# First writes to a shared stretch of SBUF placed behind the block products, and a slack test before VectorE leaves an operation to another engine

## The chip, the cores and the metric

One Trainium2 chip; the kernel runs on one of its cores. A core has five engines with a queue of their own each: TensorE (PE in the profile, its weight loads PEld), VectorE (DVE), ScalarE (ACT), GpSimd (POOL) and SyncE (SP), which issues the transfers between DRAM and SBUF here. The metric is the device time of one launch in microseconds (us); lower is better. All times are of this one core.

## The reference

One inference step of a two-layer decoder trunk, for a prompt of 512 tokens and 8 sample sequences of one token each, model width 1024, feed-forward width 4096, float32. Cut to what matters here:

```python
for l in range(DEPTH):                       # 2 layers
    u = x @ w_in[l]                          # 1024 -> 1536 columns
    A = window_attention(q, k, v)            # window 128, 8 query heads, 2 kv heads, width 512
    B = recurrent_branch(xr, gr)             # conv, RG-LRU gates, scan, width 256
    C = pool_branch(zp)                      # trailing means, width 256
    x = layer_norm(ALPHA * x + concat(A, B, C) @ w_out[l], ln1_g[l], ln1_b[l])
    x = layer_norm(ALPHA * x + square(relu(x @ w_ff1[l])) @ w_ff2[l], ln2_g[l], ln2_b[l])
```

The prompt and the sample tokens go through the same weights. The caches, shifted by one position, are outputs too.

## The kernel before, in words

**Data.** Activations lie transposed, channels on the 128 partitions and tokens along the free axis, in two halves of tokens: h=0 with 256 columns and h=1 with 256 prompt columns and the 8 samples (264). Each float32 operand of a matmul is split into a high and a low part of the fast type fp32r (`xh` and `xl`, `hh` and `hl`, two halves of a slot `w`). A product of 128 output channels is then three matmuls for each 128 input channels: high with high, low with high, high with low. Weights come by SP into two raw buffers (`raw_93`, `raw_95`), are rounded to the high part by ScalarE and subtracted by VectorE (`w<-raw,w`), and lie in seven slots `w_84` to `w_90`.

**Stages.** Each layer runs the input projection with attention, recurrence and pooling beside it, then the output projection (`do_out`, 8 chunks of 128 channels for each half), the first norm, then the feed-forward in four quarters, f1 and f2 in turn, and the second norm, whose chunks come out of the last f2. Eight pairs of f1 column blocks in a layer (`PAIRS`) are computed by 2 x 2 block products with seven instead of eight products (`do_pair`): sums of input blocks are made as fp32r and the products are combined afterwards by VectorE (`acc`, `ra`).

**The norm** (class `Norm`) takes the chunks as they come. `acc` adds them up (`acc<-y`, `acc<-acc,y`); the squares are added in two running sums. After the fourth chunk a matmul of `acc` with a matrix of 1/1024 (`x<-acc,onesm`) gives a first mean, which is then subtracted from all chunks; after the eighth a second such matmul gives the rest of the mean and `s<-over_f,onesm` the mean square. Then the chunks are normalised and split into `xh` and `xl` (`split`), or stored (`store`). In the first norm of a layer half h=0 is normalised while PE is at half h=1, and h=1 while PE is already at f1 of h=0.

**The shared stretch.** 8384 columns of SBUF have two names, `over_f` (float32) and `over_r` (fp32r). By its first name it holds, in the regions P, Q1, V, KZ, p4, long, gl0 and gl1, scratch of attention and norms: KZ is the zero-padded key buffer, which `layer_start` clears by two GpSimd MEMSETs of 64x512 at the start of each layer; "long" takes, among others, the bias of the last norm, loaded by SP in `Norm.prepare` (`over_f<-in_ln_b_dram`). By its second name it holds the input sums of the block products, in four parts T1 to T4 which cover all of it: 0 to 2112, 2112 to 4224, 4224 to 6336 and 6336 to 8384.

**Order.** Nothing is issued while the program is written down: class `Plan` records every operation (`add`), finds which earlier operations it depends on from the regions that each reads and writes, and then `order` makes a list schedule: every engine takes, from what is ready on its modelled clock, the operation with the lowest rank (the latest start that keeps the estimated end). `issue` emits them in that order, each engine keeps it as its own queue, and the waits between engines are added when the operations are emitted. As each operation is emitted from `issue`, all of them have line L319. Some operations may run on more than one engine: `either` gives an add VectorE and GpSimd, `copy` gives a ScalarE copy one or both of the others. Who takes such an operation is decided in `pick`, inside `order`: `o.eng` is the engine it was written for, `e` the one that is choosing, `free[...]` when an engine's clock is free, `o.rank + late - start` the slack. MARGIN is 3.0 us and BUSY 0.3 us.

## Time and profile before

| | before |
|---|---|
| median of 3 runs | 1107.15 us (1103.31 to 1110.06) |
| the profiled execution | 1105.39 us, its span 1103.3 us |
| mean granted TensorE clock | 0.995 |
| PE busy | 1075.4 us, 97% of the span |
| DVE busy | 796.4 us, 72% |
| ACT busy | 552.4 us, 50% |
| POOL busy | 209.6 us, 19% |

The span is the time from the first to the last instruction on the core; 2.1 us lie around it. A row of the timeline gives start, duration, engine, line, operation, out<-in, shapes, and in brackets how long the engine was idle ahead of it and who ended that. A row of the waits gives engine and operation, whom it waited for, us in total, times, and the longest.

### The profile page before, as it was taken

Reading aid. Unit: us, or ns where it says so; the run is one execution under the profiler, and the core shown is the slowest. Engines: PE = TensorE matmul, PEld = TensorE weight load, DVE = VectorE, ACT = ScalarE, POOL = GpSimd, SP = SyncE. Lnnn points to the kernel's source line nnn. Section 1 sums busy time; section 2 is a strip of 40 time slices with the busy share of each in tenths; the row PEclk is TensorE's granted clock in tenths of the full one; section 3 lists DMA queues with packets and bytes.
Section 4 is the critical chain, followed back from the end, with each engine's and each line's share of the span. In section 5 each row is a group of like instructions: output and inputs, shape, how many; then the busy total and the mean of one; then the engine's idle time right before and its main releaser. Section 6 shows DMA issues by size and latency. Waiting matters only on the chain.

```text
span 1103.3 us, 21246 instructions
## 1 busy us (share of the span) xinstructions
PE 1075.4 (97%) x8541; PEld 1046.6 (95%) x8541; DVE 796.4 (72%) x1661; ACT 552.4 (50%) x1066; POOL 209.6 (19%) x352
## 2 busy tenths in 40 slices
PE   8999999999999999999999999999999999989997
PEld 7988898999999999999998899999999999989996
DVE  5747769999559548669874596799975774675666
ACT  6658755755124224237476776566532431343343
POOL 4334334210000000022242443223000000002103
PEclk9999999999999999999999999999999999999999
DMA  9330413634313422434534040346242242242431
GB/s 266 98 76 3 114 44 116 192 120 137 111 60 98 132 77 78 124 106 155 172 89 99 1 116 5 115 144 205 77 128 67 75 153 77 78 134 83 148 116 40
DMA packets 120021, 116.58 MB, mean 106 GB/s; under 512 B 4481, under 2 KB 118171, under 8 KB 119875
## 3 DMA queue, kind: packets, MB, share of 16 engines
q1 hardware_dynamic: 119570, 115.16, 34.2%
q8 instruction: 67, 1.10, 0.4%
q14 instruction: 32, 0.25, 0.1%
q0 software_dynamic: 352, 0.06, 0.0%
HBM read 112.72 MB, written 4.84 MB: 107 GB/s over the span
## 4 chain that ended last, share of the span: by engine, by line
PE 80%; DVE 7%; ACT 5%; DMA 4%; issue 2%; SPq 1%; POOL 0%; DVEq 0%; ACTq 0%; POOLq 0%
PE mm L319 62%; PE s L319 9%; PE t L319 7%; PE x L319 2%; DVE y L319 2%; DVE over_f L319 2%; DMA raw<-in_w_ff_dram 2%; ACT L319 1%; DVE w L319 1%; DMA raw<-in_w_out_dram 1%; SPq L319 1%; ACT over_f L319 1%; ACT w L319 1%; DMA over_f<-in_x_sample_dram 1%; DVE ra L319 1%
## 5 line engine op out<-in xcount | busy, mean ns | idle before, releaser
L319 PE MATMUL mm<-hh,w 128*128 128x264 f32 (+1 forms) x2496 | 465.6, 285 | 0.8 <-ACT hh L319 0.8
L319 PE MATMUL mm<-xh,w 128*128 128x264 f32 (+1 forms) x2048 | 403.2, 290 | 1.0 <-ACT xh L319 0.9
L319 PEld LDWEIGHTS mm<-hh,w 128*128 128x128 f32 x2496 | 391.9, 190 | 2.8 <-ACT hh L319 1.4
L319 PE MATMUL mm<-hl,w 128*128 128x264 f32 (+1 forms) x1248 | 354.8, 285 | 0.4 <-DVE hl L319 0.4
L319 PEld LDWEIGHTS mm<-xh,w 128*128 128x128 f32 x2048 | 325.9, 190 | 7.1 <-issue 3.8
L319 ACT CAST w<-raw 128x1024 fp32r<-128x1024 f32 (+1 forms) x202 | 209.1, 1041 | 244.7 <-PE mm L319 204.8
L319 PE MATMUL mm<-xl,w 128*128 128x264 f32 (+1 forms) x1024 | 297.0, 290 | 0.0
L319 DVE TENSOR_TENSOR w<-raw,w 128x1024 fp32r<-128x1024 f32 (+1 forms) x202 | 247.5, 1231 | 56.6 <-ACT w L319 53.7
L319 PEld LDWEIGHTS mm<-hl,w 128*128 128x128 f32 x1248 | 237.2, 190 | 1.2 <-DVE hl L319 0.8
L319 PEld LDWEIGHTS mm<-xl,w 128*128 128x128 f32 x1024 | 194.2, 190 | 3.9 <-issue 3.4
L319 DVE TENSOR_TENSOR y<-y,mm 128x256 f32<-128x256 f32 (+1 forms) x96 | 40.5, 422 | 77.7 <-PE mm L319 77.4
L319 ACT CAST hh<-rb 128x264 fp32r<-128x264 f32 (+1 forms) x128 | 50.9, 410 | 54.6 <-DVE rb L319 54.3
L319 POOL TENSOR_SCALAR w<-four 128x512 fp32r<-128x512 f32 x4 | 2.6, 640 | 376.0 <-DVE four L319 376.0
L319 DVE TENSOR_TENSOR hl<-rb,hh 128x264 fp32r<-128x264 f32 (+1 forms) x128 | 52.4, 424 | 8.6 <-ACT hh L319 8.6
L319 PE MATMUL s<-over_r,w 128*128 128x264 f32 x384 | 53.0, 286 | 5.7 <-DMA over_f<-in_ln_b_dram 4.3
L319 PEld LDWEIGHTS s<-over_r,w 128*128 128x128 f32 x384 | 49.1, 189 | 6.3 <-DMA over_f<-in_ln_b_dram 4.6
L319 PE MATMUL t<-over_r,w 128*128 128x264 f32 (+1 forms) x384 | 51.1, 282 | 0.0
L319 PEld LDWEIGHTS t<-over_r,w 128*128 128x128 f32 x384 | 48.0, 188 | 0.0
L319 ACT CAST w<-four 128x1024 fp32r<-128x1024 f32 (+1 forms) x28 | 24.2, 866 | 41.2 <-PE mm L319 26.3
L319 ACT ACT_TABLE_LOAD x32 | 41.1, 1283 | 3.0 <-DVE nm L319 1.7
L319 ACT ACTIVATE over_f<-y 128x264 f32<-128x264 f32 (+1 forms) x49 | 19.4, 418 | 41.5 <-DVE y L319 30.0
L319 ACT ACTIVATE ra<-mm 128x256 f32<-128x256 f32 (+1 forms) x64 | 24.3, 384 | 29.9 <-PE mm L319 29.7
(288 smaller groups left out, 1346.7 us busy)
## 6 DMA issues: line engine op xcount, KB each, us to landing
raw<-in_w_ff_dram SPq DMA_DIRECT2D x80, 1024.0 KB
raw<-in_w_in_dram SPq DMA_DIRECT2D x7, 1024.0 KB
raw<-in_w_in_dram SPq DMA_DIRECT2D x8, 512.0 KB
raw<-in_w_out_dram SPq DMA_DIRECT2D x8, 512.0 KB
raw<-in_w_out_dram SPq DMA_DIRECT2D x16, 256.0 KB
y<-in_x_prompt_dram SPq DMA_DIRECT2D x4, 256.0 KB
raw<-in_w_in_dram SPq DMA_DIRECT2D x4, 256.0 KB
y<-in_x_prompt_dram SPq DMA_DIRECT2D x2, 512.0 KB
```

The lines of the kernel that those rows point to most:

```text
L319: o.ins = fn(*args, **kw)
```

## The change

Two edits.

The first is in `Plan.add`. An operation that touches the stretch under its second name (`over_r`) is remembered, and every later operation that writes the stretch under its first name gets the remembered one, the last recorded use of `over_r`, as one more dependency in the plan, whether their regions overlap or not.

The second is in `pick`. When an engine looks at an operation written for another engine, it passes over it if that other engine is free within 0.3 us. For VectorE this now holds only if the operation also has more than 3 us of slack; an urgent one it may take.

```diff
         self.alias, self.large = {}, False
+        self.second = {}
...
                 rl.append((r, op))
+            if a.name in self.alias:
+                self.second[nm] = op
+            elif w and nm in self.second:
+                deps.add(self.second[nm])
         deps.discard(op)
...
                         if e == "G":
                             if o.rank + late - start < o.alts[e][1] + MARGIN:
                                 continue
-                        elif max(free[o.eng], est) <= start + BUSY:
+                        elif max(free[o.eng], est) <= start + BUSY and (e != "V" or o.rank + late - start > MARGIN):
                             continue
```

The program has as many PE and SP instructions as before, 20 VectorE instructions more, 19 GpSimd instructions and one ScalarE instruction fewer. Three places show what moved.

PE at the last block product of layer 0, before. `t_123` and `s_144` are PSUM banks, `over_r` the input sums, `w_87` and `w_88` weight slots; in brackets the engine whose signal the instruction waits for:

```order
L319 MATMUL t_123<-over_r,w_87 128x264 x12
L319 MATMUL s_144<-over_r,w_88 128x264 [waits DVE_49]
L319 MATMUL s_144<-over_r,w_88 128x264
L319 MATMUL s_144<-over_r,w_88 128x264 [waits Pool_49]
L319 MATMUL s_144<-over_r,w_88 128x264 x6
L319 MATMUL s_144<-over_r,w_88 128x264 [waits Pool_49]
L319 MATMUL s_144<-over_r,w_88 128x264 x2
```

And in the changed kernel:

```order
L319 MATMUL t_123<-over_r,w_87 128x264 x12
L319 MATMUL s_144<-over_r,w_88 128x264 [waits DVE_49]
L319 MATMUL s_144<-over_r,w_88 128x264 x11
L319 MATMUL mm_130<-xh_113,w_86 128x256
L319 MATMUL mm_130<-xl_115,w_86 128x256
```

The matmuls are the same; the two waits for GpSimd, whose MEMSETs of KZ stood between them, are gone.

PE at the last block product of layer 1, before:

```order
L319 MATMUL t_122<-over_r,w_85 128x256 x12
L319 MATMUL s_144<-over_r,w_90 128x264 [waits Activation_49]
L319 MATMUL s_144<-over_r,w_90 128x264
L319 MATMUL s_144<-over_r,w_90 128x264 [waits DMAHW5_49]
L319 MATMUL s_144<-over_r,w_90 128x264 x9
```

In the changed kernel ten of the twelve stand in one row of eleven without a wait for a transfer. SP at the same place, as a difference:

```order
 L319 DMA raw_95<-in_w_ff_dram 128x8x256
 L319 DMA raw_93<-in_w_ff_dram 128x8x256
+L319 DMA raw_95<-in_w_ff_dram 128x8x256
 L319 DMA over_f<-in_ln_b_dram 128x1024
-L319 DMA raw_95<-in_w_ff_dram 128x8x256
 L319 DMA raw_93<-in_w_ff_dram 128x8x256
 L319 DMA raw_95<-in_w_ff_dram 128x8x256
```

The load of the bias stands one weight load later.

VectorE in the first norm of layer 0, before. `y_0_92` and `xh_113`, `xl_115` are of half h=0, which is being normalised, `y_0_94` and `acc_157` of half h=1, whose chunks are still coming, `pcol_98` holds gains and biases:

```order
L319 TENSOR_TENSOR y_0_92<-y_0_92,over_f 128x256
L319 SCALAR_TENSOR_TENSOR over_f<-y_0_92,pcol_98,over_f 128x256 x2
L319 CAST xh_113<-over_f 128x256
L319 TENSOR_TENSOR w_84<-raw_93,w_84 128x1024
L319 SCALAR_TENSOR_TENSOR xl_115<-over_f,pcol_98,xh_113 128x256
L319 SCALAR_TENSOR_TENSOR over_f<-y_0_92,pcol_98,over_f 128x256 x2
L319 TENSOR_TENSOR w_85<-raw_95,w_85 128x1024
L319 SCALAR_TENSOR_TENSOR xl_115<-over_f,pcol_98,xh_113 128x256
L319 TENSOR_TENSOR w_86<-raw_95,w_86 128x1024
L319 SCALAR_TENSOR_TENSOR over_f<-y_0_92,pcol_98,over_f 128x256
L319 SCALAR_TENSOR_TENSOR xl_115<-over_f,pcol_98,xh_113 128x256
L319 TENSOR_TENSOR acc_157<-acc_157,y_0_94 128x264
```

And in the changed kernel, from the first of two adds to the second:

```order
L319 TENSOR_TENSOR acc_157<-acc_157,y_0_94 128x264
L319 SCALAR_TENSOR_TENSOR over_f<-over_f 128x256
L319 TENSOR_TENSOR y_0_92<-y_0_92,over_f 128x256
L319 SCALAR_TENSOR_TENSOR over_f<-over_f 128x256
L319 TENSOR_TENSOR y_0_92<-y_0_92,over_f 128x256
L319 SCALAR_TENSOR_TENSOR over_f<-over_f 128x256
L319 TENSOR_TENSOR y_0_92<-y_0_92,over_f 128x256
L319 SCALAR_TENSOR_TENSOR over_f<-y_0_92,pcol_98,over_f 128x256
L319 COPY y_0_94<-mm_130 128x264
L319 TENSOR_TENSOR acc_157<-acc_157,y_0_94 128x264
```

The last add ahead of the first mean stood behind three weight splits (`w_84` to `w_86`); now it stands ahead of them, and VectorE makes the copy before it, which ScalarE made.

PE at the same place, as a difference (`x_149` is the bank of the mean, `mm_128` an output chunk):

```order
 L319 MATMUL mm_128<-hh_0_126,w_86 128x264 x2
 L319 MATMUL mm_128<-hl_0_127,w_86 128x264
+L319 MATMUL x_149<-acc_157,onesm_100 128x264
 L319 MATMUL mm_128<-hh_0_126,w_86 128x264 x2
 L319 MATMUL mm_128<-hl_0_127,w_86 128x264
```

The first mean matmul of half h=1 is the 1107th matmul on PE instead of the 1168th, 61 earlier; the second, at the end of the chunks, is the 1212th instead of the 1259th, 47 earlier. Layer 1 has the same moves.

Elsewhere: the four copies of the sample caches to the output (`out_dram<-in_cache_k_dram` and three more) stand one weight load earlier on SP in both layers; in whole, the adds `acc<-acc,y` of 128x264 are 5 on GpSimd and 19 on VectorE, which were 16 and 8.

## The prediction

> **What bounds the kernel now.** I read the page's totals first, then PE's waits, then the timeline at each long wait, and at last busy time and clock by stretch.

> ```profile
> span 1103.3 us, 21246 instructions
> PE 1075.4 (97%) x8541; PEld 1046.6 (95%) x8541; DVE 796.4 (72%) x1661; ACT 552.4 (50%) x1066; POOL 209.6 (19%) x352
> PE 80%; DVE 7%; ACT 5%; DMA 4%; issue 2%; SPq 1%; POOL 0%; DVEq 0%; ACTq 0%; POOLq 0%
> ```

> TensorE (PE) is busy for 1075.4 of 1103.3 us and carries 80% of the chain that ended last. The change takes no matmul away, so it can win only from the 27.9 us in which PE is idle and from stretches in which PE's clock is low. Who ends PE's idle time:

> ```profile
> PE x L319 <- DVE acc L319: 6.4, 5, 1.8
> PE s L319 <- DMA over_f<-in_ln_b_dram: 4.3, 1, 4.3
> PE t L319 <- DMA y<-in_x_prompt_dram: 3.6, 1, 3.6
> PE t L319 <- DVE over_f L319: 1.7, 2, 1.1
> PE s L319 <- POOL over_f L319: 1.3, 2, 0.7
> ```

> The columns are us in total, times, longest. Rows two and five (block products `s<-over_r` that wait for something written to `over_f`) are what the first edit speaks to: 5.6 us. Row one (mean matmuls `x<-acc` that wait for VectorE's sum) is what the second edit can reach. Rows three and four stand at the start and in the sample attention, whose work neither edit shortens.

> **Edit 1, the ordering.** In layer 0's last block product two MEMSETs of KZ come between the matmuls:

> ```profile
> 443.96 0.52 POOL L319 MEMSET over_f<- 64x512 f32 x1 [22.27 <-PE s L319]
> 444.54 1.13 PE L319 MATMUL s<-over_r,w 128*128 128x264 f32 x7 [0.70 <-POOL over_f L319]
> 445.73 0.52 POOL L319 MEMSET over_f<- 64x512 f32 x1 [1.24 <-PE s L319]
> 446.30 0.64 PE L319 MATMUL s<-over_r,w 128*128 128x264 f32 x3 [0.63 <-POOL over_f L319]
> ```

> PE reads, POOL writes, PE reads on: each MEMSET is one wait. In the new order both MEMSETs stand behind the last product, and the matmuls have no wait on POOL. That frees 0.70 + 0.63 = 1.33 us. KZ is wanted only by the next layer's attention, after the f2 pass that begins here, and POOL is idle for 22.27 us ahead of the first, so what they cost there is hidden; without that cover it would be 2 x 0.52 = 1.04 us.

> In layer 1 it is the DMA of the ln2 bias:

> ```profile
> 984.24 0.35 SPq L319 DMA_DIRECT2D over_f<-in_ln_b_dram  x1
> 988.50 1.94 PE L319 MATMUL s<-over_r,w 128*128 128x264 f32 x10 [4.34 <-DMA over_f<-in_ln_b_dram]
> 984.30:988.50 4.20, 0.00 (x0) 0.00 (x0) 1.43 (x4) 1.45 (x2) 0.00 (x0) 1.00 0.69 188
> 989.30:992.70 3.40, 3.40 (x18) 3.40 (x17) 2.22 (x4) 1.05 (x1) 0.00 (x0) 0.50 0.41 143
> 993.00:997.00 4.00, 4.00 (x35) 4.00 (x35) 3.37 (x8) 1.71 (x3) 0.00 (x0) 1.00 0.16 32
> ```

> The last three rows are stretches: length, then busy time of PE, PE's weight loads, DVE, ACT, POOL, then granted clock, DMA share, GB/s. PE does nothing for 4.2 us, and then runs 3.4 us at a granted clock of 0.50: 18 matmuls, where the pitch of the next stretch (4.00/35 = 0.114 us) would give 30. Twelve matmuls are lost, 12 x 0.114 = 1.4 us. If the stall goes, I expect the low clock to go with it: 4.34 + 1.4 = 5.74 us. [...]

> The bias load moves behind one weight load on SP's queue, and waits there for the last block product; no matmul stands behind it. The bias is used when the output is stored, at the end of the f2 pass that begins here, and the one weight load that stood behind it is now issued ahead of it. Cost 0; if SP's next load were held up by it, at most about the 4.2 us that PE now stands still for it.

> Edit 1 together: 1.33 + 5.74 = 7.1 us, the upper end; the lower is the stalls alone, 1.33 + 4.34 = 5.7.

> **Edit 2, the slack rule.** So far VectorE (DVE) passed over another engine's operation whenever that engine was soon free; now it does so only where the operation has over 3 us of slack, and takes urgent ones. In the first norm of each layer VectorE gains 6 instructions and POOL loses 5 (among them three adds to `acc_157`), and the mean matmuls stand 61 and 47 matmuls earlier on PE. Here is what they wait for now:

> ```profile
> 178.50 0.68 PE L319 MATMUL x<-acc,onesm 128*128 128x264 f32 x2 [0.98 <-DVE acc L319]
> 191.31 0.71 PE L319 MATMUL x<-acc,onesm 128*128 128x264 f32 x2 [1.40 <-DVE acc L319]
> 714.20 0.68 PE L319 MATMUL x<-acc,onesm 128*128 128x264 f32 x2 [0.97 <-DVE acc L319]
> 727.35 0.71 PE L319 MATMUL x<-acc,onesm 128*128 128x264 f32 x2 [1.75 <-DVE acc L319]
> 160.00:195.00 35.00, 32.56 (x259) 31.67 (x257) 31.84 (x57) 19.72 (x39) 14.63 (x14) 1.00 0.34 107
> 195.00:255.00 60.00, 59.40 (x496) 58.99 (x494) 58.44 (x116) 38.93 (x79) 9.97 (x9) 1.00 0.50 160
> ```

> The most that can be won is 0.98 + 1.40 + 0.97 + 1.75 = 5.1 us. VectorE is busy 31.84 of 35 us there and 58.44 of the next 60, so it is nearly the bound itself. Does the sum come sooner? It depends on where it stands in VectorE's queue:

> ```profile
> 163.31 0.42 DVE L319 TENSOR_TENSOR over_f<-s,over_f 128x256 f32<-128x256 f32 x1
> 163.64 0.62 DVE L319 TENSOR_TENSOR y<-y,over_f 128x256 f32<-128x256 f32 x1
> 165.97 0.81 POOL L319 TENSOR_TENSOR acc<-acc,y 128x264 f32<-128x264 f32 x1 [1.10 <-DVE y L319]
> 166.08 0.97 DVE L319 TENSOR_TENSOR y<-y,over_f 128x256 f32<-128x256 f32 x1
> 168.57 0.36 ACT L319 COPY y<-mm 128x264 f32<-128x264 f32 x1
> 177.93 0.42 DVE L319 TENSOR_TENSOR acc<-acc,y 128x264 f32<-128x264 f32 x1
> 179.73 1.22 DVE L319 TENSOR_TENSOR w<-raw,w 128x1024 fp32r<-128x1024 f32 x1
> 188.01 0.94 POOL L319 TENSOR_TENSOR acc<-acc,y 128x264 f32<-128x264 f32 x1
> 190.84 0.42 DVE L319 TENSOR_TENSOR acc<-acc,y 128x264 f32<-128x264 f32 x1
> ```

> The fourth chunk of y, the last that the first mean needs, was copied by 168.93 and added only at 177.93: the add stood behind nine us of weight splits and other norm work in VectorE's queue. In the new order the add is the 11th instruction behind the variance step (163.31 now), which has two more ahead of it than now. The pitch is 0.33 us (163.31 to 163.64). So the step starts at 163.31 + 0.66 = 164.0, and with two instructions stretched by 0.97 - 0.42 = 0.55 the add starts at 164.0 + 11 x 0.33 + 1.1 = 168.7 and ends at 169.2. PE came to the mean at 178.50 - 0.98 = 177.52. A matmul takes 60/496 = 0.121 us in the stretch from 195, so 61 fewer in front bring PE there at 177.52 - 7.4 = 170.1: 0.9 us to spare.

> For the second mean PE came at 191.31 - 1.40 = 189.91, and comes 47 x 0.121 = 5.7 sooner, less the 0.98 won: 183.2. The squares and adds now run on POOL until 188.95 and on VectorE until 191.26, among weight splits (w, 1.22 each). In the new order 29 small instructions and one split stand between the first mean's add and the last add of the second: 169.2 + 29 x 0.33 + 1.2 and, as a guess, four stretched by 0.55, gives 182.2: 1.0 us to spare. Layer 1's order is the same.

> What it costs VectorE: an add takes 426 ns on VectorE and 816 on POOL, and operations of one shape are stretched where POOL works beside them:

> ```profile
> L319 POOL TENSOR_TENSOR acc<-acc,y 128x264 f32<-128x264 f32 x16 | 13.1, 816 | 15.9 <-DVE y L319 14.2 <-DVE acc L319 1.7
> L319 DVE TENSOR_TENSOR over_f<-over_f 128x264 f32<-128x264 f32 x15 | 11.9, 794 | 0.0
> L319 DVE TENSOR_TENSOR acc<-acc,y 128x264 f32<-128x264 f32 x8 | 3.4, 426 | 0.3
> ```

> Six more instructions are 6 x 0.33 = 2.0 us; five fewer on POOL give back at most 5 x (794 - 426) = 1.8. VectorE comes out even, within its 3.16 + 1.56 = 4.7 us of idle time in 160 to 255. [...]

> Both margins are about 1 us on chains of a dozen instructions, and one stretched instruction takes 0.55 of it. I take two thirds of 5.1: 3.5 us. The ends: 5.1 gained, or a loss, priced with the rivals.

> The other moves: four copies of the sample caches to the output stand one weight load earlier on SP.

> ```profile
> 228.20 0.63 SPq L319 DMA_DIRECT2D out_dram<-in_state_conv_dram  x1
> 249.47 0.38 SPq L319 DMA_DIRECT2D raw<-in_w_ff_dram  x1
> ```

> No load is issued for 21 us behind them, so the displaced load has room: 0. In layers' ends and attention a handful of casts change engine, each some 0.4 us off PE's path: 0, within 1 us either way.

> **Sum.** 7.1 + 3.5 = 10.6 us. The profiled execution took 1105.39 us (span 1103.3 and 2.1 around it): 1094.8. The median of the three runs is 1107.15, 1.8 higher: 1096.6. I predict 1095.5, between them.

> **Rivals.**
> Only edit 1 pays: the sums come sooner, but PE, which meets them sooner too, waits as long as now. Then 1105.39 - 7.1 = 1098.3, or 1100.1 by the median. For it: VectorE 91 to 97% busy there. Against: the 9 us in which the finished chunk lay unused.

> The other side: PE takes its instructions in order, and the mean matmuls stand 61 and 47 earlier. If VectorE finishes the sums only when it does now, PE waits 7.4 + 5.7 = 13.1 us more per layer: 1105.39 - 7.1 + 26.2 = 1124.5. The gain of edit 1 is used up when the sums come 3.5 us per layer behind PE beyond today's waits; slower by 0.5% (5.5 us) needs 6.3. It would take, say, the six new instructions at 1 us each with none of the idle time usable. For it: instructions near 1 us do occur (0.97 above). Against: the queue position as counted.

> The ordering does nothing, because something else holds the same matmuls (a sum from VectorE, a weight): then only edit 2, 1105.39 - 3.5 = 1101.9. Against: VectorE has gaps and PE waits for nothing else in those rows.

> The clock drops elsewhere. It does now, once, after short gaps:

> ```profile
> 666.49 0.24 PE L319 MATMUL t<-ident,over_f 64*128 64x64 f32 x1 [0.64 <-DVE over_f L319]
> 668.50:671.80 3.30, 3.30 (x15) 3.01 (x14) 1.90 (x5) 0.68 (x2) 1.24 (x3) 0.50 0.00 0
> ```

> [...]

> **How the numbers follow.** Both edits pay, 1091.5 to 1098: 0.58. Only edit 1, 1098 to 1101.5: 0.22. The means give back most or all of it, 1101.5 to 1112: 0.12. Beyond that, slower: 0.04. Ordering without effect: 0.04. Best case 1105.39 - 7.1 - 5.1 - 1.4 = 1091.8, and 1.5 lower for the spread of runs: low 1090.3. High 1102: it takes in edit 1 alone by the median (1100.1) with one clock drop more. A measurement of this kernel can tell about 0.5%, 5.5 us, from no change: faster holds the first two cases but for their edge, 0.78; same 0.17; slower 0.05.

> **What would show it.** In the new profile no wait of `s<-over_r` for POOL or for the bias load; no granted clock of 0.50 behind the last block product of layer 1; `x<-acc` waits down from 6.4 to under 3 us in total; the VectorE adds `acc<-acc,y` 128x264 from 8 to 19 and POOL's from 16 to 5. PE's busy time stays near 1075 less the slow stretch. The prediction is wrong if `x<-acc` waits grow past 6.4, if waits for `hh`, `hl` or `w` appear from 195 on, or if weight loads (`raw`) come late and end PE's idle time.

## The result, and the profile after

The changed kernel took 1097.64 us (median of 7 runs, 1094.60 to 1103.00), the kernel before 1105.24 us in the same comparison (7 runs, 1103.18 to 1111.38): a ratio of 0.9927, 95% interval 0.9902 to 0.9952, so 0.5 to 1.0% faster. Times and ratios in this text leave out two single executions far from all others, 3716.55 us of e9 and 1303.65 us of e10. The profiled execution took 1097.64 us, with a span of 1095.9. In its code the line of every operation is L324, in the kernels of the last experiments L335.

Totals and PE's waits of the changed kernel:

```profile
PE 1073.0 (98%) x8541; PEld 1045.8 (95%) x8541; DVE 796.4 (73%) x1681; ACT 550.3 (50%) x1065; POOL 195.2 (18%) x333
...
PE t L324 <- DMA y<-in_x_prompt_dram: 4.8, 1, 4.8
PE mm L324 <- ACT hh L324: 4.1, 2, 2.5
PE mm L324 <- ACT xh L324: 1.8, 1, 1.8
PE t L324 <- DVE over_f L324: 1.3, 2, 0.7
PE s L324 <- DVE nm L324: 1.2, 1, 1.2
PE mm L324 <- DVE hl L324: 1.1, 3, 0.6
PE x L324 <- ACT rb L324: 1.1, 1, 1.1
```

Both groups of waits that the edits speak to are gone: no `s<-over_r` that waits for POOL or for the bias, no `x<-acc` that waits for VectorE. Of the five such waits of before (6.4 us) four were at the first norms and are gone (5.1); the fifth, in the last norm of the kernel (1.32 us, at 1090.86 in before), is still there with 1.08 us, and now stands under ScalarE (`x<-ACT rb`). At the start of f2 two others have grown: `mm` for `hh` and for `hl`, which were in before:

```profile
PE mm L319 <- ACT hh L319: 0.8, 2, 0.4
PE mm L319 <- DVE hl L319: 0.4, 2, 0.2
```

The two last block products, layer 0 and layer 1, in the timeline:

```profile
445.71 1.49 PE L324 MATMUL s<-over_r,w 128*128 128x264 f32 x11
...
982.37 1.63 PE L324 MATMUL s<-over_r,w 128*128 128x264 f32 x12
983.38 0.37 SPq L324 DMA_DIRECT2D raw<-in_w_ff_dram  x1
984.08 0.35 SPq L324 DMA_DIRECT2D over_f<-in_ln_b_dram  x1
```

The twelve matmuls run through, and the bias is issued behind them. Where the new waits stand, by stretches of 3.41 us (PE, its weight loads, DVE, ACT and POOL busy, clock, DMA share, GB/s):

```profile
737.24:740.65 3.41, 3.33 (x28) 3.09 (x26) 3.41 (x7) 3.41 (x7) 0.00 (x0) 1.00 0.68 228
740.65:744.06 3.41, 0.66 (x3) 0.30 (x2) 2.65 (x6) 2.66 (x6) 1.87 (x1) 1.00 0.52 182
744.06:747.47 3.41, 3.10 (x14) 3.10 (x15) 3.23 (x5) 2.29 (x5) 3.38 (x3) 0.50 0.38 128
```

This is the start of f2 in layer 1: PE is nearly idle for a stretch (0.66 us busy of 3.41), and then has half its clock for another (0.50 from 744.06 to 747.47).

To see where time comes and goes, I compare the start of the n-th matmul in two traces. Each trace has 8541 of them, and outside the places that were reordered the same number is the same work. A stage's entry is what the difference to the trace of before changed by between two such numbers (us, negative is gained). The numbers that bound the stages are 0 to 800 (start), 800 to 1200 (sample attention of layer 0), 1200 to 1460 (means), 1460 to 1800 (start of f2), 3300 to 3600 (last block product), 5000 to 5300, 5300 to 5660 and 5660 to 6000 (the same three of layer 1), 7500 to 7900 (the bias). "All" is for the last matmul; the stretches that have no column make up the rest.

| trace | start | sample 0 | means 0 | f2 0 | MEMSETs | sample 1 | means 1 | f2 1 | bias | all |
|---|---|---|---|---|---|---|---|---|---|---|
| changed kernel | 2.44 | 1.31 | -3.26 | 1.78 | -1.91 | -1.49 | -3.38 | 4.15 | -6.15 | -8.14 |
| e1 edit 1 | 1.30 | -0.27 | -0.19 | -0.01 | -1.91 | -1.57 | -0.50 | -0.04 | -6.15 | -9.32 |
| e2 edit 2 | 0.88 | -0.36 | -3.25 | 3.57 | -0.01 | 3.01 | -3.37 | 1.99 | -0.23 | -0.14 |
| e3 both | 0.15 | -0.43 | -3.25 | 2.89 | -1.91 | -1.65 | -3.37 | 1.82 | -6.15 | -13.33 |
| e4 GpSimd's only | 1.03 | 1.35 | -1.31 | 0.04 | -1.91 | 0.15 | -2.80 | 1.00 | -6.15 | -9.91 |
| e5 bias only | 0.23 | 1.85 | -0.17 | -0.01 | 0.00 | -0.01 | 0.62 | -0.04 | -6.15 | -5.12 |
| e6 MEMSETs only | 0.48 | -0.32 | 0.13 | -0.01 | -1.91 | -1.45 | -0.56 | -0.04 | 0.95 | -2.65 |
| e7 half a bias | 0.27 | 1.39 | -0.26 | -0.03 | 0.00 | -0.19 | -0.62 | -0.02 | 0.41 | 1.55 |
| e8 tail first | -0.09 | -0.09 | -3.30 | 0.13 | -1.91 | -1.47 | -3.40 | 0.04 | -6.15 | -15.54 |
| e9 edit 1, tail | 1.48 | -0.27 | -0.19 | 0.84 | -1.91 | -1.13 | -0.58 | 0.83 | -6.15 | -8.34 |
| e10 as e8 | 0.95 | 0.31 | -3.26 | 0.25 | -1.91 | 3.34 | -3.38 | -0.16 | -6.15 | -8.88 |
| e11 e4 with tail | 0.86 | 4.96 | -1.73 | 0.02 | -1.91 | -1.07 | -2.88 | 1.22 | -6.15 | -8.31 |

Two columns repeat to the hundredth wherever edit 1 is whole, MEMSETs and bias; the means repeat within 0.05 wherever edit 2 is whole. The sample columns do not: they swing from -1.65 to 4.96, and between two traces of one kernel too (-1.47 in e8, 3.34 in e10). That is chiefly the granted clock (in the second sample column three windows at 0.50 in e10, none in e8), at the end of this text. Of the stretches without a column one shows edit 2 as well: between 3600 and 5000, at the start of layer 1, the traces with it gain 0.76 to 1.02 us, those without it are between -0.42 and 0.28.

### The profile page after: what moved, and what is told of

Its sections match the earlier page's. It is cut to its first block, busy times and chain, and to the rows that moved or that the text cites. A ratio compares the mean times of both kernels' runs of the same rounds, so it can differ in the third digit from the quotient of the medians.

```text
span 1095.9 us, 21224 instructions
## 1 busy us (share of the span) xinstructions
PE 1073.0 (98%) x8541; PEld 1045.8 (95%) x8541; DVE 796.4 (73%) x1681; ACT 550.3 (50%) x1065; POOL 195.2 (18%) x333
## 4 chain that ended last, share of the span: by engine, by line
PE 79%; DVE 8%; DMA 6%; ACT 4%; SPq 1%; issue 1%; DVEq 0%; ACTq 0%
PE mm L324 62%; PE s L324 9%; PE t L324 6%; DMA raw<-in_w_ff_dram 2%; DVE w L324 2%; PE x L324 2%; DMA raw<-in_w_out_dram 2%; DVE over_f L324 2%; DMA raw<-in_w_in_dram 2%; DVE y L324 1%; ACT L324 1%; SPq L324 1%; ACT w L324 1%; ACT over_f L324 1%; DVE rb L324 1%
## 5 line engine op out<-in xcount | busy, mean ns | idle before, releaser
L324 PE MATMUL mm<-hh,w 128*128 128x264 f32 (+1 forms) x2496 | 467.6, 286 | 4.2 <-ACT hh L324 4.1
L324 PE MATMUL mm<-xh,w 128*128 128x264 f32 (+1 forms) x2048 | 400.8, 290 | 1.8 <-ACT xh L324 1.8
L324 PEld LDWEIGHTS mm<-hh,w 128*128 128x128 f32 x2496 | 393.1, 190 | 6.2 <-ACT hh L324 4.8
L324 PE MATMUL mm<-hl,w 128*128 128x264 f32 (+1 forms) x1248 | 355.7, 285 | 1.1 <-DVE hl L324 1.1
L324 ACT CAST w<-raw 128x1024 fp32r<-128x1024 f32 (+1 forms) x202 | 208.0, 1040 | 258.6 <-PE mm L324 207.5
L324 PEld LDWEIGHTS mm<-xh,w 128*128 128x128 f32 x2048 | 324.5, 189 | 7.4 <-issue 3.8
L324 PE MATMUL mm<-xl,w 128*128 128x264 f32 (+1 forms) x1024 | 296.4, 289 | 0.0
L324 DVE TENSOR_TENSOR w<-raw,w 128x1024 fp32r<-128x1024 f32 (+1 forms) x202 | 247.8, 1235 | 60.1 <-ACT w L324 58.2
L324 PEld LDWEIGHTS mm<-hl,w 128*128 128x128 f32 x1248 | 237.8, 191 | 2.1 <-DVE hl L324 1.7
L324 PEld LDWEIGHTS mm<-xl,w 128*128 128x128 f32 x1024 | 193.5, 189 | 4.1 <-issue 3.4
L324 DVE TENSOR_TENSOR y<-y,mm 128x256 f32<-128x256 f32 (+1 forms) x96 | 40.4, 421 | 76.6 <-PE mm L324 76.6
L324 ACT CAST hh<-rb 128x264 fp32r<-128x264 f32 (+1 forms) x128 | 51.1, 409 | 49.6 <-DVE rb L324 49.3
L324 POOL TENSOR_SCALAR w<-four 128x512 fp32r<-128x512 f32 x4 | 2.6, 638 | 376.1 <-DVE four L324 376.1
L324 DVE TENSOR_TENSOR hl<-rb,hh 128x264 fp32r<-128x264 f32 (+1 forms) x128 | 53.9, 433 | 8.4 <-ACT hh L324 8.3
L324 PE MATMUL s<-over_r,w 128*128 128x264 f32 x384 | 51.8, 284 | 0.0
L324 PE MATMUL t<-over_r,w 128*128 128x264 f32 (+1 forms) x384 | 51.1, 282 | 0.0
L324 PEld LDWEIGHTS s<-over_r,w 128*128 128x128 f32 x384 | 48.5, 188 | 0.0
L324 PEld LDWEIGHTS t<-over_r,w 128*128 128x128 f32 x384 | 48.0, 188 | 0.0
L324 ACT CAST w<-four 128x1024 fp32r<-128x1024 f32 (+1 forms) x28 | 24.2, 865 | 43.9 <-PE mm L324 26.3
L324 ACT ACTIVATE ra<-mm 128x256 f32<-128x256 f32 (+1 forms) x64 | 24.5, 382 | 36.1 <-PE mm L324 36.1
L324 DVE TENSOR_TENSOR w<-four,w 128x1024 fp32r<-128x1024 f32 (+1 forms) x32 | 30.5, 954 | 10.7 <-ACT w L324 10.5
```

Source lines behind the costliest of these rows:

```text
L324: o.ins = fn(*args, **kw)
```

## The experiments

**Each edit alone, and both on the same chip.** e1 has the first hunk of the diff, e2 the second, e3 both.

> Edit 1 alone. Theory A (the trace of after: edit 1 carries the whole gain, edit 2 gives back at the start of f2 what it wins at the means): 8 us faster than before, ratio about 0.993; no wait of s<-over_r for POOL or the bias load, x<-acc waits stay at 5 or 6 us, the wait of mm for hh at the start of f2 stays under 1 us. Theory B (each edit pays a part, as forecast): 5 to 7 us faster, ratio 0.994 to 0.996, clearly slower than the kernel with both edits.

> Edit 2 alone. Theory A: within 2 us of before, ratio 0.998 to 1.002; x<-acc waits near 0, the mm waits for hh and hl at the start of f2 together 4 to 6 us, and the waits of s<-over_r stay at 5.6. Theory B: 3.5 us faster, ratio 0.997, with hh waits near 1.

> Both edits, as the changed kernel, on the same chip as the two alone. Theory A: ratio as of edit 1 alone within 0.002 (about 0.993). Theory B: lower than edit 1 alone by 0.003.

Against the same runs of before (median 1107.17): e1 1095.87, ratio 0.9895 (0.9863 to 0.9927); e2 1104.73, 0.9971 (0.9950 to 0.9991); e3 1094.94, 0.9890 (0.9855 to 0.9926). Both edits are no faster than edit 1 alone, as far as 0.35% can be told. Theory A's outline stands: edit 1 carries the gain. Its figures do not all: for e1 it had 0.993, just outside the interval, and the 11 us that the ratio says are more than the 8.06 that the trace shows at edit 1's two places; where the others come from is not shown. Its "within 2 us of before" for e2 is missed too: the ratio says 3.2 us (1.0 to 5.5), which is theory B's 3.5, while the waits (`hh` 3.2 and `hl` 1.3) are the 4 to 6 us of theory A. By the table edit 2 wins 3.3 us at the means of each layer, and gives 1.8 to 2.0 back at f2 where the clock holds at 1.00 and 2.9 to 4.2 where it drops (to 0.50 for 3.41 us in the changed kernel, above). Expectation B's clear difference between e1 and e3 was not there.

PE's waits of e1 and e2:

```profile
PE x L319 <- DVE acc L319: 4.7, 4, 1.3
...
PE mm L319 <- DVE hl L319: 1.5, 2, 0.7
```

```profile
PE s L319 <- DMA over_f<-in_ln_b_dram: 4.3, 1, 4.3
...
PE mm L319 <- ACT hh L319: 3.2, 2, 1.6
...
PE s L319 <- POOL over_f L319: 1.3, 2, 0.7
```

Each edit removes its own waits; the waits for `hh` come with edit 2.

**The slack rule for GpSimd's operations only.**

```diff
-... and (e != "V" or o.rank + late - start > MARGIN):
+... and (e != "V" or o.eng != "G" or o.rank + late - start > MARGIN):
```

> Both edits, but the slack rule of edit 2 only for operations written for GpSimd, so that ScalarE's copies of y and casts stay on ScalarE. Theory A in its plain form (the adds alone pull the norm ahead and starve the end of f1): x<-acc waits near 0 and hh waits of 4 to 5 us as with both edits, ratio about 0.993. Rival C (the copies of y that moved from ScalarE to VectorE, and the casts of xh that went the other way, make ScalarE late for hh): hh waits under 1.5 us, 3 us faster than both edits.

1094.25 us, ratio 0.9874 (0.9846 to 0.9901), not to be told from e3. The plain form of theory A falls on one point and rival C on the gain: the waits for `hh` are indeed gone, but others come instead.

```profile
PE mm L319 <- DVE hl L319: 2.2, 4, 1.2
PE mm L319 <- ACT xh L319: 1.9, 1, 1.9
PE mm L319 <- POOL xl L319: 1.5, 2, 1.1
```

The means win only 1.31 and 2.80 us net, since PE waits for `xl` from GpSimd inside that stage. In these two kernels, which copies move decides which operand is late, not whether one is.

**Edit 1 in its two halves.** In `Plan.add` the added dependency is given only to writes by SP (e5), or only to the others (e6):

```diff
-            elif w and nm in self.second:
+            elif w and nm in self.second and eng == "P":    # e5; e6: eng != "P"
```

> Edit 1 only for writes by a transfer (the bias of layer 1), the MEMSETs left as before, edit 2 not made. If edit 1's gain is the sum of independent waits: PE gains 6.15 us between matmul 7600 and 8000 against before (4.34 of stall and the rest low clock) and nothing between 3400 and 3600, where the two waits for POOL stay at 1.3. Rival: another writer of the stretch takes the place of the bias, and the gain is under 3.

> Edit 1 only for the other writers (the MEMSETs of KZ), the bias load left as before, edit 2 not made. Independent waits: 1.9 us gained between matmul 3400 and 3600, none between 7600 and 8000, where PE waits 4.3 for the bias and runs 3.4 us at a granted clock of 0.50. The rival of e5 has no gain there either.

Each was run once. e5 gains 6.15 us at the bias and 0.00 at the MEMSETs, where both waits for POOL stay (0.70 and 0.63); e6 gains 1.91 at the MEMSETs and keeps the stall of 4.3, with two stretches of low clock behind it instead of one (0.50 from 983.36 to 990.19; 0.95 lost). The halves are independent and add up to e1; the rival falls.

**Half a bias.** The kernel before, but only 512 of the bias's 1024 columns are loaded, and used for both halves of the output:

```diff
-                dma(out=t, in_=ln2_b[self.l].partition_broadcast(128))
+                t = t[:, :512]
+                dma(out=t, in_=ln2_b[self.l, 0:512].partition_broadcast(128))
...
```

> The kernel before, but only the first 512 of the 1024 columns of the bias are loaded and used for both halves of the output. The stall should shrink from 4.34 to about 3 us. If the clock drops only behind an idle window of 3.4 us, it stays at 1.00 there and the place gains 1.3 + 1.4 = 2.7 us against before; if a stretch of 3.41 us on a fixed grid that is about half idle is enough, the drop comes still, or not, by where the grid falls, and the place gains 1.3 or 2.7.

```profile
988.66 1.69 PE L319 MATMUL s<-over_r,w 128*128 128x264 f32 x6 [3.68 <-DMA over_f<-in_ln_b_dram]
984.28:987.69 3.41, 0.70 (x6) 0.49 (x5) 2.56 (x5) 1.87 (x4) 0.00 (x0) 1.00 0.38 119
987.69:991.10 3.41, 2.44 (x11) 2.44 (x12) 0.00 (x0) 0.05 (x1) 0.00 (x0) 0.50 0.90 309
991.10:994.52 3.42, 3.42 (x17) 3.42 (x17) 2.85 (x6) 0.99 (x1) 0.00 (x0) 0.50 0.00 1
```

In this one run the wait shrank from 4.34 only to 3.68, not to 3: half the bytes took 0.66 us off, so by an estimate from these two figures about 3 us of such a stall are not its bytes. The two conditions that the expectation sets for the clock can be told apart here, although 3.68 is over 3.4: the wait began at 984.98 (988.66 less 3.68), and the clock fell at 987.69, after 2.71 us of it. An idle stretch of 3.4 us was not needed. The clock fell to 0.50 for two stretches (6.83 us) instead of one, and the place lost 0.41 us although its stall was shorter.

**The tail of f1 first.** Where does f2's wait come from? ScalarE and VectorE in e3 at the f1 to f2 switch of layer 0, and PE's wait:

```profile
204.17 0.91 ACT L324 ACTIVATE y<-over_f,pcol 128x264 f32<-128x264 f32 x2
204.98 0.40 ACT L324 CAST hh<-rb 128x256 fp32r<-128x256 f32 x1
205.28 0.42 ACT L324 CAST xh<-y 128x264 fp32r<-128x264 f32 x1
205.59 1.05 ACT L324 CAST w<-raw 128x1024 fp32r<-128x1024 f32 x1
206.54 0.38 ACT L324 ACTIVATE ra<-mm 128x256 f32<-128x256 f32 x1
206.81 1.04 ACT L324 CAST w<-raw 128x1024 fp32r<-128x1024 f32 x1
206.96 0.96 DVE L324 TENSOR_TENSOR rb<-ra 128x256 f32<-128x256 f32 x1
207.75 0.42 ACT L324 CAST xh<-y 128x264 fp32r<-128x264 f32 x1
208.06 0.41 ACT L324 CAST hh<-rb 128x256 fp32r<-128x256 f32 x1
208.53 0.50 PE L324 MATMUL mm<-hh,w 128*128 128x256 f32 x2 [1.62 <-ACT hh L324]
```

The last chunk of f1 (`ra` at 206.54, then `rb`, `hh`) stands in ScalarE's queue behind casts and activations of the norm of half h=1 (`y<-over_f`, `xh<-y`) and a weight's cast. Such work stands there in before, too (a cast of `w` at 206.47, `y` at 207.42). But PE now comes there 3.5 us sooner (matmul 1460 of e3 against before), and the `hh` that it needs only 2.2 us (208.06, where it was 210.25). In e8 the operations of that last chunk are marked, and each is moved, in two passes, ahead of up to three earlier operations of its engine, in the finished order:

```diff
...
+        for o in 2 * [o for o in done if o.first]:
+            i = done.index(o)
+            j, n = i - 1, 0
+            while n < 3 * (o.first > 1):
+                q = done[j]
+                if q.eng == o.eng:
+                    if q.first or q in o.deps or any(x in q.succ for x in done[j + 1:i + 1]):
+                        break
+                    done.insert(i, done.pop(j))
+                    i, n = i - 1, n + 1
+                j -= 1
...
```

> Both edits, and in each engine's final order the chain of the last f1 chunk of half h=0 in the first quarter (ra, rb, hh, hl) is moved ahead of up to three operations of its engine that stand in front of it (weight splits, casts of xh and adds of the norm of half h=1). Theory A (the norm that now ends sooner puts its casts and the weight splits in front of that chain at the start of f2): the wait of 1.78 us per layer for hh shrinks by 1 to 1.7, no other wait takes its place, 2 to 3 us less than both edits in the PE's times, ratio to before 0.986 to 0.987. Rival D (VectorE and ScalarE are simply full there, and what is pushed back is missed at once): the waits for hl, xl or w grow by as much, and the kernel is as both edits, 0.989.

1092.01 us, ratio 0.9859 (0.9827 to 0.9890). f2's start loses 0.13 and 0.04 us instead of 1.8 and more: that the work queued ahead of this chain makes the wait is shown. That the earlier norm put it there, as theory A says, is not: part of it stood there before.

```profile
206.91 0.39 PE L335 MATMUL mm<-hl,w 128*128 128x256 f32 x1 [0.44 <-DVE hl L335]
207.68 0.51 PE L335 MATMUL mm<-hh,w 128*128 128x256 f32 x2 [0.27 <-ACT hh L335]
```

But some of it comes back, though not at once, as rival D had it: between the matmuls 1800 and 3300, and 6000 and 7500, where no kernel with another order differs from before, this one loses 1.25 and 0.74 us.

```profile
272.40 2.00 ACT L335 CAST w<-raw 128x1024 fp32r<-128x1024 f32 x2 [1.60 <-DMA raw<-in_w_ff_dram]
274.30 0.40 ACT L335 CAST hh<-rb 128x256 fp32r<-128x256 f32 x1
274.75 0.38 PE L335 MATMUL mm<-hh,w 128*128 128x256 f32 x1 [0.65 <-ACT hh L335]
```

PE now arrives before the weights: ScalarE waits 1.60 us for a weight load (0.21 at this cast in e3), and `hh` is queued behind that cast.

**Is it the tail or edit 2?** e9 is e8 without edit 2, e10 is e8 again, e11 is e8 with the rule of e4.

> Edit 1 and the reordered tail of f1 of e8, without edit 2. Theory A (edit 2's gain at the means is real and was only hidden by the tail of f1): the means still wait, 2.5 to 2.9 us per layer, the tail has only 0.9 us per layer to win, so 1 to 2 us less than edit 1 alone and 2 to 4 us more than e8; ratio 0.988 to 0.989. Rival E (edit 2 is worth nothing, the reordered tail alone makes e8's gain): as e8, 0.986.

> The kernel of e8 again, on the same chip as e9: 0.986, the f2 waits 1.0 us per layer, and 2 to 4 us less than e9 by theory A, the same by rival E.

> As e8, but the slack rule only for operations written for GpSimd. In e4 this form had 0.5 to 1.4 us waits for hl at the start of f2 and 0.6 to 1.7 us waits for xl from GpSimd per layer. The reordered tail should take 1 us per layer of the first and none of the second: 0.986 to 0.987, not faster than e10.

Against the same runs of before (median 1106.09): e9 1098.50, ratio 0.9921 (0.9892 to 0.9950); e10 1094.13, 0.9886 (0.9858 to 0.9914); e11 1095.49, 0.9882 (0.9850 to 0.9914). e9 is 4.4 us slower than e10 in the medians, on the same chip; its five runs (1097.06 to 1101.65) all lie above the five of e10 (1093.88 to 1096.20). That is theory A's order, but its ratio for e9, 0.988 to 0.989, is missed: the tail did not win 0.9 us per layer. Without edit 2 the new order costs 0.83 us per layer, because `hl` then waits behind two weight splits and an operation of the norm (2.35 and 0.97 us on VectorE):

```profile
213.74 0.39 PE L335 MATMUL mm<-hl,w 128*128 128x256 f32 x1 [1.68 <-DVE hl L335]
```

So the tail alone is not the gain; rival E falls. Of the difference between e9 and e10 the means are 5.9 us and the starts of f2 1.6, and other stages took part of it back. e10's 0.9886 missed its 0.986: its f2 starts are near those of e8 (0.25 and -0.16), but the sample attention of layer 1 cost 3.34 where e8 won 1.47, and 1.77 instead of 1.25 came back later. e11 met its expectation in not being faster than e10 and missed the rest: the tail took nothing off its waits for `hl` (2.7 us in all, 2.2 in e4), and the ratio is above 0.987. Whether the reordered tail beats the changed kernel is not settled: 0.9859 and 0.9886 stand against 0.9890 and 0.9927, from different chips, and the intervals overlap.

## Why the prediction was right or wrong

The forecast was 1095.5 in 1090.3 to 1102.0; it came to 1097.64, faster as forecast. The total lies in the range, though the gain is 7.6 us by the medians where the sum had 10.6. Of the two terms one was too small, and the other left out a loss; that the two errors partly cancel is luck. So is the case that it fell in: 1097.64 is inside "both edits pay" (to 1098) by 0.4 us, while e1 and e3 say that edit 2 adds nothing that can be told on top of edit 1.

Edit 1, forecast 7.1 with 7.1 as its upper end, won 1.91 + 6.15 = 8.06. The mechanism was as described, and the moved MEMSETs and load cost nothing that shows: apart from the start, which lies ahead of both places and differs by up to 2.5 us among all the kernels, no column of e1 lost. The dependency was a false one: the last block product reads T1, columns 0 to 2112 of the stretch, while KZ lies at 3616 to 4640 and the bias at 6752 to 7776. The term mis-sized is the price of a stall: the wait that stands in the row of a matmul (0.70 + 0.63) is less than PE loses. The row counts from the end of the last matmul, and matmuls overlap (0.28 us long, one every 0.12); the weight loads' rows show 0.91 and 0.85 for the same two waits. For the bias e1 wins 4.50 us up to the first matmul behind the stall and 1.65 in the low clock, which was counted as 1.4.

Edit 2, forecast 3.5 out of at most 5.1, won 3.26 + 3.38 = 6.6 at the means. The "at most" was too low for the same reason: from start to start the four mean matmuls of before came 1.26, 1.68, 1.25 and 2.03 us after the matmul ahead of them, where 0.12 is usual, which makes 5.7. The count of the queue held for the first mean: at matmul 1200 the changed kernel ran 3.75 us later than before, so it was due at 170.1 + 3.75 = 173.85; it started at 173.51 and did not wait. For the second it held only just:

```profile
173.51 0.61 PE L324 MATMUL x<-acc,onesm 128*128 128x264 f32 x2
185.98 0.43 DVE L324 TENSOR_TENSOR acc<-acc,y 128x264 f32<-128x264 f32 x1
186.54 0.65 PE L324 MATMUL x<-acc,onesm 128*128 128x264 f32 x2
```

The sum was there at 186.41, 0.1 us ahead of PE, where the prediction had 1.0 to spare. The 0.1 is the same in all five traces with edit 2 whole.

The step that failed is "VectorE comes out even" as a reason to look no further: it weighed VectorE's total, and not what would stand at the next narrow place when the norm ended sooner. f2's start, where `hh` and `hl` waited 0.6 us per layer before, took back 1.78 + 4.15 = 5.9 of the 6.6. It was named only as a sign that the prediction was wrong (waits for `hh`, `hl` or `w` "from 195 on"), and had no price. Counted, it would have made edit 2 worth about 1 us in the trace, and the likeliest case the rival "only edit 1 pays" (1098.3 to 1100.1), though not by that rival's own reason: the means no longer wait. e2 came out 3.2 us faster (1.0 to 5.5), near the 3.5 of the forecast, as a larger win less a loss that was not counted.

The rival of the in-order means (1124.5) did not come: the sums were there. That the ordering does nothing is refuted by e5 and e6. The clock drop that comes and goes was worth more than the 1.4 us that each end of the range has for one drop: the sample stages differ by up to 5 us (4.96 in e11).

VectorE did come out even, 796.4 us busy before and after with 20 instructions more; 19 adds on VectorE and 5 on GpSimd, as the order had it. Its adds are not at 426 ns but at 500:

```profile
L324 DVE TENSOR_TENSOR acc<-acc,y 128x264 f32<-128x264 f32 x19 | 9.5, 500 | 0.7
L324 POOL TENSOR_TENSOR acc<-acc,y 128x264 f32<-128x264 f32 x5 | 4.4, 876 | 4.9 <-DVE y L324 3.2 <-DVE acc L324 1.7
```

## What to carry to other kernels

Here a false dependency between two names of one memory cost the engine that waited more than the rows of the waits show: 8.1 us for 5.7 us of listed waits, 1.65 of it by the low clock behind one of them. When a wait is taken away, ask what the engine meets next, now sooner, and whether the queues that feed it there come as much sooner, and price that place; here the waits that were small there (`hh` 0.8 and `hl` 0.4 us) are the ones that grew (4.1 and 1.1). For stages that a chance effect disturbs, compare the start of the same matmul in two traces: stages that repeat to 0.01 us can then be told from those that do not.

## What the runs showed of the hardware

```profile
663.15:666.56 3.41, 2.25 (x13) 1.81 (x14) 2.91 (x10) 2.83 (x6) 1.45 (x2) 1.00 0.00 0
666.56:669.97 3.41, 3.41 (x16) 3.12 (x15) 1.99 (x6) 1.72 (x4) 0.66 (x3) 0.50 0.00 0
669.97:673.39 3.42, 3.42 (x17) 3.42 (x18) 0.56 (x2) 2.56 (x5) 0.00 (x0) 0.50 0.00 0
673.39:676.80 3.41, 3.41 (x18) 3.41 (x18) 1.39 (x5) 0.99 (x2) 0.00 (x0) 0.50 0.02 5
676.80:680.20 3.40, 3.40 (x29) 3.35 (x29) 2.75 (x8) 0.39 (x1) 0.32 (x1) 1.00 0.00 0
```

All seven drops after 12 to 15 matmuls came in the sample attention, where two short waits (0.42 to 1.10 and 0.48 us) lie near each other: whether they fall into one window or two depends on where the grid stands in that run. In before those of layer 1 (0.64 and 0.48) lie in one window (665.05 to 668.46, 13 matmuls), and the clock is 0.50 in the next; between those of layer 0 (1.07 and 0.48) a window ends, at 132.57, and the clock stays at 1.00. In the first sample column the five traces with a drop there (the changed kernel, e4, e5, e7, e11) have 1.31 to 4.96, the others -0.43 to 0.31; in the second, where before has a drop itself, those without one have -1.07 to -1.65 and those with one that lasts three windows (e2, e10) 3.01 and 3.34. So the clock makes most of the swing of these columns; whether it makes the spread between runs of one kernel was not tested. Shortening those two waits was not tried; it is the next thing that the traces point to.
